# Gathered activations spread between gathered rows, eight row buffers and seven load buffers in a two-layer decoder trunk

## The chip, the cores and the metric

The kernel runs as one program on one core of a Trainium2 chip. The metric is device microseconds of one execution; the time before is the median of three runs. The profiler recorded one further execution, and its trace is what is read below. Engine names are those of the profile: PE is the matrix engine and PEld its weight loads, DVE the vector engine, ACT the scalar engine, POOL the GpSimd engine, SP the sync engine, which here issues nearly all weight loads from DRAM.

## The reference

Two layers, 256 tokens, width 1024, all float32. Each layer has a mixing part (projection, windowed attention, a short convolution, a gated mixer, output projection) and a retrieval part called PEER. The change lies in PEER:

```python
def block(t):                                   # t: tokens x 1024
    q = (t @ w_pq).reshape(T, 8, 2, 128)
    s = einsum('thpk,hpnk->thpn', q, sub_keys)  # two times 128 key scores per head
    # top 16 of each half, top 16 of the 256 sums: 8 heads x 16 experts per token
    gate = softmax(best_s)
    u = expert_down[experts]                    # 16384 experts of 1024
    act = gelu(einsum('td,thkd->thk', t, u))
    vv = expert_up[experts]
    return einsum('thk,thkd->td', gate * act, vv)
x = x + gate2 * peer_ffn(h2)
```

## The kernel before

**Two ways to sum the experts.** Instead of gathering 128 experts for each of 256 tokens, the kernel streams both expert tables, 128 tiles of 128 experts each, through the PE. The *first product* multiplies every `down` tile with all 256 tokens and leaves GELU activations for all experts. For the first `T` = 192 tokens a gate for every expert is made from one-hot matrices (`make_onehots`, `gate_mm`), and the gated activations `acts` stay in SBUF. The *second product* (`combine`) streams the 128 `up` tiles and accumulates `acts` times `up` in four PSUM banks.

**The last 64 tokens.** For the other `TS` = 64 tokens the second product covers only part of the work in matrix form: their ungated activations are written to DRAM (`act_rows`) in the first product. In the second product POOL issues, for each of 64 steps k, an indirect DMA that gathers one expert row of 1024 floats on each of 128 partitions (`fetch`, 512 KB, a *row* below), and another that gathers 64 activations on each partition (`fetch_acts`, 32 KB, an *act* below). For every group of eight acts DVE makes eight weights (`weights`, three instructions), and for every row it does one multiply and add over 128x1024 (`add_row`).

**Order in the second product.** It is written by hand (a manual schedule); elsewhere the compiler's scheduler sets the order on each engine. The PE works through tile i with ten matmuls of 128x512, six with the high part of the split `up` tile and four with its low part. Ahead of it ACT casts the raw tile to its high part (`hi`), and DVE subtracts to get the low part (`lo`); `hi` and `lo` have three buffers each, so both run about two tiles ahead of the PE. Every fourth tile, `split` prepares four tiles of `acts`: two casts on ACT and one subtraction on DVE. In the same DVE queue stand the row additions, spread evenly from tile `F_FIRST` to tile `F_LAST` by `want`, and the weights. DVE, POOL and PE each take their queue in order, so an addition that waits for its row holds up the `lo` behind it, and with it the PE.

**Buffers.** Raw tiles of all weight streams share one pool of `RAW` = 5 buffers, which SP refills in order (`dma_ahead`). Rows have `RING` = 4 buffers, so the fetch of row k + 4 stands behind the addition of row k. Acts have two halves of eight. POOL's queue at that place is: 4 rows, 24 acts, then eight rows and eight acts in turn. In layer 0, at tile 84, `tables` also puts three loads and a masking instruction for the next layer into the POOL queue, and at tile 92 the residual stream is read back from DRAM on it.

Of the kernel before, what the change touches and what calls it, by code (L numbers as in the profile page):

```python
# [11 lines left out]
F16 = mybir.dt.float16  # L12
# [5 lines left out]
P = 128  # L18
# [11 lines left out]
NP = 64  # L30
RAW = 5
AHEAD = 300
# [12 lines left out]
TS = S - T  # L45
RING = 4
GROUP = 8
F_FIRST = 9
F_LAST = 126
# [8 lines left out]
def hybrid_trunk(ctx: ExitStack, tc: tile.TileContext, x_in, c_in, vec_in, w_ada, w_in, w_out, w_pq,  # L58
# [82 lines left out]
    R_T = region(64 * S, 2, D)  # L141
    R_ROWS = region(96 * S, RING, D)
    R_SUM = region(112 * S, D)
# [769 lines left out]
    def experts(layer, rest):  # L913
# [3 lines left out]
        def make_onehots(g):  # L917
            tile4 = work.tile([P, 4, 4 * P], F16, name="oh", tag="oh", bufs=2)
            oh = tile4[:, 0].rearrange("p (i n) -> p i n", i=4)
# [59 lines left out]
        def split(q):  # L979
# [3 lines left out]
            for i in range(4 * q, 4 * q + 4, n):  # L983
# [6 lines left out]
                for k in range(n):  # L990
                    splits[i + k] = hi[:, k, :P], lo[:, k, :P], slot[:, k, T + P:2 * T + TS]

        def combine(layer, late):

# [5 lines left out]
            acc = {p: bank("acc", 4) for p in turns}  # L1000
            rows = up.rearrange("l j i c -> (l j i) c")
            where_act, where_row, w8 = (R_IX[:, n, :] for n in range(3))
            fetched = added = 0

            def fetch(k):
                nc.gpsimd.indirect_dma_start(  # L1006
                    out=R_ROWS[:, k % RING, :], out_offset=None, in_=rows,
                    in_offset=bass.IndirectOffsetOnAxis(ap=where_row[:, k:k + 1].bitcast(U32), axis=0))

            def fetch_acts(g):  # L1010

                for k in range(g * GROUP, (g + 1) * GROUP):
                    nc.gpsimd.indirect_dma_start(  # L1013
                        out=R_ACTS[:, k % (2 * GROUP), :], out_offset=None, in_=act_rows[layer][:, :],
                        in_offset=bass.IndirectOffsetOnAxis(ap=where_act[:, k:k + 1].bitcast(U32), axis=0))

# [8 lines left out]
            def add_row(k):  # L1025
                v = R_ROWS[:, k % RING, :]
                if k == 0:
                    nc.vector.tensor_scalar(R_SUM, v, w8[:, 0:1], None, op0=OP.mult)
                else:
                    nc.vector.scalar_tensor_tensor(R_SUM, v, w8[:, k:k + 1], R_SUM, op0=OP.mult, op1=OP.add)  # L1030
# [9 lines left out]
            split(0)  # L1040
            nc.vector.tensor_copy(where_act.bitcast(U32), pairs[:, 0, :])
            nc.vector.tensor_scalar(where_row.bitcast(U32), pairs[:, 0, :], float(layer * P * P), None, op0=OP.add)
            split(1)
            while fetched < RING:
                fetch(fetched)
                fetched += 1
            fetch_acts(0)
            fetch_acts(1)
            for i in range(128):
# [4 lines left out]
                while added < want(i):  # L1054
                    add_row(added)
                    added += 1
                    if fetched < TS:
                        fetch(fetched)
                        fetched += 1
                g = -(-want(i + 2) // GROUP) - 1  # L1060
                if i >= F_FIRST - 2 and g > -(-want(i + 1) // GROUP) - 1:
                    weights(g)
                    if 1 < g + 2 < TS // GROUP:
                        fetch_acts(g + 2)
                if i == 127 and layer + 1 < DEPTH:
# [61 lines left out]
        for i in range(128):  # L1127
# [21 lines left out]
            elif start is not None:  # L1149
# [3 lines left out]
                while sent < want and len(waiting) < 2:  # L1153
                    waiting.append((sent, gate_mm(sent)))
                    sent += 1
                    if made < NG:
                        make_onehots(made)
                        made += 1
            if j == 1:
                tdone = 4 * gdone  # L1160
                pend = (pair, act(pair, ps, tdone), tdone)
# [101 lines left out]
```

## Time and profile before

| What | Value |
|---|---|
| Median of the runs | 1806.55 us (three runs, 1805.11 to 1808.86) |
| The profiled execution | 1808.34 us, its span in the trace 1806.6 us |
| Granted PE clock, mean of the span | 0.987 |
| Busy share of the span | PE 96%, PEld 87%, DVE 79%, ACT 50%, POOL 48% |
| DRAM traffic | 454.48 MB, 252 GB/s on average |
| Second product of layer 0 | from 582.0 us to 916.3 us of the span |
| Second product of layer 1 | from 1468.1 us to 1795.5 us of the span |

The difference of 1.7 us between the execution's own time and its span lies before the first and after the last recorded instruction. A group's row in the page gives line, engine, operation, output and input by the program's names, count, busy time and mean duration, and the idle time ahead of it with what ended it. Many buffers are regions of one large tile named `arena`, so that name alone does not tell rows from acts: the line does (before, L1006 fetches rows, L1013 fetches acts, L1030 adds rows, L1021 to L1023 make weights, L229 makes `lo`, L236 makes `hi`, L989 is the subtraction of `split`, L1034 is the second product on the PE).

### The profile page before, as it was taken

How to read it: one execution, taken by the hardware profiler on the slowest of the kernel's cores; microseconds unless marked ns; L12 is line 12 of the kernel's file. 1: busy time of each engine (PE TensorE's matmuls, PEld its weight loads, DVE VectorE, ACT ScalarE, POOL GpSimd, SP SyncE). 2: the span in 40 equal slices, each digit the busy share in tenths (PEclk: the TensorE clock that was granted, in tenths of full speed). 3: DMA queues.
4: the chain of work that ended last, by engine and by line, in shares of the span. 5: the costliest groups of instructions: out<-in, count | busy, mean ns of one | idle time of the engine just before them, and what ended most of it. 6: DMA issues, size and time to landing. Idle time of an engine off the chain costs nothing.

```text
span 1806.6 us, 32055 instructions
## 1 busy us (share of the span) xinstructions
PE 1734.2 (96%) x11848; PEld 1578.5 (87%) x11848; DVE 1433.9 (79%) x2679; ACT 905.6 (50%) x1469; POOL 870.6 (48%) x697
## 2 busy tenths in 40 slices
PE   7999999999999899998999999999999997998898
PEld 6789999999999677776888999999999996877787
DVE  5868998888998588886966699957777857977896
ACT  2445455544445354554656555545544454545453
POOL 1000204779994765775400011317777746777641
PEclk9999999999999999998999999999999999999999
DMA  9865568887887798999943446666665677988895
GB/s 368 309 230 175 172 209 283 263 261 252 259 262 242 254 328 320 330 320 332 365 153 127 164 164 186 201 194 200 191 201 190 197 258 247 338 305 316 317 389 189
DMA packets 159279, 454.48 MB, mean 252 GB/s; under 512 B 50513, under 2 KB 50897, under 8 KB 157970
## 3 DMA queue, kind: packets, MB, share of 16 engines
q1 hardware_dynamic: 99936, 363.38, 59.0%
q0 software_dynamic: 23936, 80.50, 12.2%
q10 hardware_dynamic: 35250, 8.56, 2.2%
q8 instruction: 93, 1.52, 0.3%
q14 instruction: 64, 0.52, 0.1%
HBM read 440.75 MB, written 11.54 MB: 250 GB/s over the span
## 4 chain that ended last, share of the span: by engine, by line
PE 76%; DVE 9%; issue 5%; DMA 4%; POOL 4%; ACT 1%; SPq 0%; DVEq 0%; POOLq 0%; ACTq 0%
PE acc L1034 22%; PE ch L308 14%; PE ch L309 14%; PE ch L310 14%; POOL arena L1013 3%; DVE lo L229 3%; PE ch L306 2%; DMA arena<-in_up,arena 2%; PE g L938 1%; PE g L939 1%; PE ch L388 1%; DMA raw<-in_w_ada 1%; PE acc L308 1%; PE acc L310 1%; PE acc L309 1%
## 5 line engine op out<-in xcount | busy, mean ns | idle before, releaser
L236 ACT CAST hi<-raw 128x1024 fp32r<-128x1024 f32 x554 | 581.5, 1050 | 715.1 <-PE ch L310 367.2
L229 DVE TENSOR_TENSOR lo<-raw,hi 128x1024 fp32r<-128x1024 f32 x554 | 676.4, 1230 | 154.2 <-ACT hi L236 138.5
L308 PE MATMUL ch<-hh,hi 128*128 128x256 f32 x2336 | 666.1, 285 | 0.0
L309 PE MATMUL ch<-hh,lo 128*128 128x256 f32 x2336 | 658.6, 282 | 0.2 <-DVE lo L229 0.2
L310 PE MATMUL ch<-hh,hi 128*128 128x256 f32 x2336 | 657.8, 282 | 0.0
L925 POOL TENSOR_SCALAR oh<-iota,picks 128x128 f16<-128x128 f16 x384 | 429.8, 1136 | 258.1 <-issue 148.3
L309 PEld LDWEIGHTS ch<-hh,lo 128*128 128x128 f32 x2336 | 440.3, 188 | 0.8 <-DVE lo L229 0.6
L308 PEld LDWEIGHTS ch<-hh,hi 128*128 128x128 f32 x2336 | 439.8, 188 | 0.3 <-issue 0.3
L310 PEld LDWEIGHTS ch<-hh,hi 128*128 128x128 f32 x2336 | 439.9, 188 | 0.0
L1034 PE MATMUL acc<-hi,hh 128*128 128x512 f32 x1536 | 411.6, 403 | 19.3 <-DVE hh L989 17.0
L1034 PEld LDWEIGHTS acc<-hi,hh 128*128 128x128 f32 x1536 | 295.4, 193 | 91.8 <-DVE hh L989 19.2
L1034 PE MATMUL acc<-lo,hh 128*128 128x512 f32 x1024 | 288.5, 403 | 27.9 <-DVE lo L229 27.9
L1006 POOL DMA_INDIRECT arena<-in_up,arena x128 | 193.2, 1509 | 199.6 <-DVE arena L1030 126.7
L1034 PEld LDWEIGHTS acc<-lo,hh 128*128 128x128 f32 x1024 | 196.4, 193 | 78.6 <-DVE lo L229 33.1
L1030 DVE SCALAR_TENSOR_TENSOR arena<-arena 128x1024 f32<-128x1024 f32 x126 | 161.6, 1283 | 79.5 <-DMA arena<-in_up,arena 79.5
L1013 POOL DMA_INDIRECT arena<-act_rows,arena x128 | 204.3, 1596 | 40.6 <-issue 33.5
L194 DVE SCALAR_TENSOR_TENSOR raw<-raw,arena 128x1024 f32<-128x1024 f32 x96 | 117.2, 1223 | 16.6 <-DMA raw<-in_w_ada 10.7
L784 POOL CAST arena<-arena 128x512 f16<-128x512 uint32 x32 | 29.2, 926 | 139.8 <-DVE arena L773 108.0
L748 POOL DMA_DIRECT2D arena<-in_keys x2 | 1.1, 563 | 155.5 <-DVE ra L324 100.8
L930 DVE TENSOR_TENSOR oh<-oh,parts 128x512 f16<-128x512 f16 x192 | 75.9, 438 | 0.0
L928 DVE TENSOR_TENSOR oh<-iota,parts 128x512 f16<-128x512 f16 x96 | 41.5, 434 | 35.5 <-PE g L939 29.5
L989 DVE TENSOR_TENSOR hh<-arena,hh 128x768 fp32r<-128x768 f32 (+1 forms) x66 | 61.3, 929 | 0.6 <-ACT hh L987 0.3
(232 smaller groups left out, 1602.4 us busy)
## 6 DMA issues: line engine op xcount, KB each, us to landing
raw<-in_down SPq DMA_DIRECT2D x256, 512.0 KB
raw<-in_up SPq DMA_DIRECT2D x256, 512.0 KB
raw<-in_w_ada SPq DMA_DIRECT2D x96, 512.0 KB
raw<-in_w_pq SPq DMA_DIRECT2D x32, 512.0 KB
raw<-in_w_in SPq DMA_DIRECT2D x26, 512.0 KB
raw<-in_w_out SPq DMA_DIRECT2D x16, 512.0 KB
act_rows<-ungated ACTq DMA_DIRECT2D x128, 64.0 KB
arena<-in_w_in SPq DMA_DIRECT2D x6, 512.0 KB
```

What stands on the lines that cost most here:

```text
L194: op = nc.vector.scalar_tensor_tensor(raw, raw, 1.0, cact, op0=OP.mult, op1=OP.mult, accum_out=mods[layer][:, col:col + 1])
L229: nc.vector.tensor_sub(lo, raw, hi.bitcast(F32))
L236: nc.scalar.copy(hi, raw)
L308: nc.tensor.matmul(dst, hi[:, cols], k[0], start=start, stop=False, **kw)
L309: nc.tensor.matmul(dst, lo[:, cols], k[0], start=False, stop=False, **kw)
L310: nc.tensor.matmul(dst, hi[:, cols], k[1], start=False, stop=stop, **kw)
L925: nc.gpsimd.tensor_scalar(oh[:, i, :], iota, picks[:, t:t + 1], None, op0=OP.is_equal)
L930: nc.vector.tensor_tensor(og[j], on, wide(1 + j), op=OP.mult)
L1006: nc.gpsimd.indirect_dma_start(out=R_ROWS[:, k % RING, :], out_offset=None, in_=rows, in_offset=bass.IndirectOffsetOnAxis(ap=where_row[:, ...
L1013: nc.gpsimd.indirect_dma_start(out=R_ACTS[:, k % (2 * GROUP), :], out_offset=None, in_=act_rows[layer][:, :], in_offset=bass.IndirectOffse ...
L1030: nc.vector.scalar_tensor_tensor(R_SUM, v, w8[:, k:k + 1], R_SUM, op0=OP.mult, op1=OP.add)
L1034: nc.tensor.matmul(acc[piece], w, u[:, lo:hi], start=piece not in opened, stop=last, skip_group_check=True)
```

## The change

- An act is fetched behind each row: step k issues row k + 4 (later k + 8) and then act k + 16. The first 16 acts are fetched in a run at the start of the second product.
- The first four rows are fetched in the first product, in code that stands at its tile 108, together with the two small DVE instructions (`where`) that make the addresses.
- Rows have four buffers up to tile 24 and eight from there on. The four new ones lie where the `acts` of the first 22 tiles were, which `split` has used up by then; at tile 24 four more rows are fetched at once.
- The two one-hot buffers move from the work pool into the arena, where the row sum and the acts lie later. The room in the pool goes to two more raw buffers, seven in place of five.
- The additions begin at tile 10 in place of 9.

```diff
-RAW = 5
+RAW = 7
-RING = 4
-F_FIRST = 9
+F_FIRST = 10
-    R_ROWS = region(96 * S, RING, D)
+    R_ROWS = [region(at * S, D) for at in (96, 100, 104, 108, 0, 4, 8, 12)]
+    R_ON = [region(at * S, D).bitcast(F16).rearrange("p (k c) -> p k c", k=4) for at in (112, 116)]
...
         def make_onehots(g):
-            tile4 = work.tile([P, 4, 4 * P], F16, name="oh", tag="oh", bufs=2)
+            tile4 = R_ON[g % 2]
...
+        free = deque(range(4))
+        slots = []
+        def fetch():
+            k = len(slots)
+            if free and k < TS:
+                slots.append(free.popleft())
+                nc.gpsimd.indirect_dma_start(
+                    out=R_ROWS[slots[k]], out_offset=None, in_=rows,
+                    in_offset=bass.IndirectOffsetOnAxis(ap=where_row[:, k:k + 1].bitcast(U32), axis=0))
+        def fetch_act(k):
+            if k < TS:
+                nc.gpsimd.indirect_dma_start(
+                    out=R_ACTS[:, k % (2 * GROUP), :], out_offset=None, in_=act_rows[layer][:, :],
+                    in_offset=bass.IndirectOffsetOnAxis(ap=where_act[:, k:k + 1].bitcast(U32), axis=0))
...
         def combine(layer, late):
             split(0)
-            nc.vector.tensor_copy(where_act.bitcast(U32), pairs[:, 0, :])
-            nc.vector.tensor_scalar(where_row.bitcast(U32), pairs[:, 0, :], float(layer * P * P), None, op0=OP.add)
             split(1)
-            while fetched < RING:
-                fetch(fetched)
-                fetched += 1
-            fetch_acts(0)
-            fetch_acts(1)
+            for k in range(2 * GROUP):
+                fetch_act(k)
...
                 while added < want(i):
                     add_row(added)
+                    free.append(slots[added])
+                    fetch()
+                    fetch_act(added + 2 * GROUP)
                     added += 1
-                    if fetched < TS:
-                        fetch(fetched)
-                        fetched += 1
+                if i == 24:
+                    free.extend(range(4, 8))
+                    for _ in range(4):
+                        fetch()
                 if i >= F_FIRST - 2 and g > -(-want(i + 1) // GROUP) - 1:
                     weights(g)
-                    if 1 < g + 2 < TS // GROUP:
-                        fetch_acts(g + 2)
...
         # first product
+            if i == 108:
+                where()
+                for _ in range(4):
+                    fetch()
```

How this moves the queues. POOL, layer 0, from the end of the retrieval part to the first rows of the second product, before (L883 saves the residual stream, L784 and L925 serve the retrieval and the one-hots, L1006 fetches a row, L1013 an act):

```order
L883 DMA x_dram<-arena 128x2048
L784 CAST arena<-arena 128x512 x16
L925 TENSOR_SCALAR oh<-iota,picks 128x128 x192
L1006 DMA arena<-in_up,arena 128x1024 x4
L1013 DMA arena<-act_rows_102,arena 128x64 x24
L1006 DMA arena<-in_up,arena 128x1024 x8
L1013 DMA arena<-act_rows_102,arena 128x64 x8
```

And now (L1007 fetches a row, L1014 an act):

```order
L883 DMA x_dram<-arena 128x2048
L784 CAST arena<-arena 128x512 x16
L925 TENSOR_SCALAR arena<-iota,picks 128x128 x12
L1007 DMA arena<-in_up,arena 128x1024 x4
L925 TENSOR_SCALAR arena<-iota,picks 128x128 x180
L1014 DMA arena<-act_rows_102,arena 128x64 x16
L1007 DMA arena<-in_up,arena 128x1024
L1014 DMA arena<-act_rows_102,arena 128x64
```

The scheduler puts the first four rows much earlier than tile 108, behind the first 12 of 192 one-hot instructions; the second product opens with 16 acts, and from there row and act alternate, where 24 acts stood in a run.

POOL, layer 0, around the loads for the next layer (L458 to L463), before:

```order
L1006 DMA arena<-in_up,arena 128x1024 x8
L1013 DMA arena<-act_rows_102,arena 128x64 x8
L1006 DMA arena<-in_up,arena 128x1024 x2
L458 DMA arena<-in_rel_bias 128x2048
L459 DMA arena<-in_sgu_w 128x512
L460 DMA arena<-in_sgu_b 128x256
L461 AFFINE_SELECT arena<-arena 128x512
L463 MEMSET arena 128x2x2
L1006 DMA arena<-in_up,arena 128x1024 x4
```

And now:

```order
L1007 DMA arena<-in_up,arena 128x1024
L1014 DMA arena<-act_rows_102,arena 128x64
L458 DMA arena<-in_rel_bias 128x2048
L459 DMA arena<-in_sgu_w 128x512
L460 DMA arena<-in_sgu_b 128x256
L461 AFFINE_SELECT arena<-arena 128x512
L463 MEMSET arena 128x2x2
L1007 DMA arena<-in_up,arena 128x1024
```

The loads stand at the same tile; around them rows and acts alternate, and the first fetch behind them is that of row 50, which waits for the addition of row 42.

DVE, layer 0, where the addresses are made (`where`; L1041 and L1042 before, L999 and L1000 now). Before, at the start of the second product, between the subtractions of `split` (L989):

```order
L229 TENSOR_TENSOR lo<-raw,hi 128x1024
L989 TENSOR_TENSOR hh<-arena,hh 128x2x192 x2
L1041 CAST arena<-pairs 128x64
L1042 TENSOR_SCALAR arena<-pairs 128x64
L989 TENSOR_TENSOR hh<-arena,hh 128x4x192
L974 TENSOR_TENSOR arena<-arena,gt 128x384
```

And now, early in the first product, at the end of the retrieval part (L850 makes the expert numbers `chosen`, from which ACT and a small DMA make `pairs`):

```order
L229 TENSOR_TENSOR lo<-raw,hi 128x1024
L850 SCALAR_TENSOR_TENSOR chosen<-arena 128x128
L229 TENSOR_TENSOR lo<-raw,hi 128x1024
L194 SCALAR_TENSOR_TENSOR raw,mod_109<-raw,arena 128x1024
L855 COPY picks<-g 128x128
L229 TENSOR_TENSOR lo<-raw,hi 128x1024
L859 SCALAR_TENSOR_TENSOR parts<-g,parts 128x128
L999 CAST arena<-pairs 128x64
L1000 TENSOR_SCALAR arena<-pairs 128x64
```

The two instructions moved ahead by most of the first product, to a place shortly behind the DMA that they wait for.

More of the change, by code (lines that the diff above doesn't have):

```diff
@@ L991, in split, with where @@
                     splits[i + k] = hi[:, k, :P], lo[:, k, :P], slot[:, k, T + P:2 * T + TS]
+        rows = up.rearrange("l j i c -> (l j i) c")
+        where_act, where_row, w8 = (R_IX[:, n, :] for n in range(3))
+        free = deque(range(4))
+        slots = []
+        def where():
+            nc.vector.tensor_copy(where_act.bitcast(U32), pairs[:, 0, :])
+            nc.vector.tensor_scalar(where_row.bitcast(U32), pairs[:, 0, :], float(layer * P * P), None, op0=OP.add)
+        def fetch():
[10 more added lines that the diff above has]
+                    in_offset=bass.IndirectOffsetOnAxis(ap=where_act[:, k:k + 1].bitcast(U32), axis=0))
         def combine(layer, late):
@@ L1000, in combine @@
             acc = {p: bank("acc", 4) for p in turns}
[L1001 to L1015, printed above, removed]
+            added = 0
             def weights(g):
@@ L1025, in add_row @@
             def add_row(k):
-                v = R_ROWS[:, k % RING, :]
+                v = R_ROWS[slots[k]]
                 if k == 0:
```

## The prediction

> **What bounds the kernel now.** I read the windows by stage first, then the waits and the PE's timeline within the stage that loses time. The first answer below counts the second product's matmuls alone (length of the window, PE busy and count, PEld, granted clock, DMA share, GB/s). The second is the PE's timeline at a stretch without loss (start of a tile's first group, 28 tiles apart) and at one stall.
>
> ```profile
> 582.00:916.30 334.30, 309.22 (x1278) 246.73 (x1278) 0.96 0.89 316
> 1468.10:1795.50 327.40, 305.11 (x1276) 243.75 (x1276) 0.97 0.86 309
> 846.00:912.00 66.00, 66.00 (x285) 53.52 (x284) 1.00 0.94 345
> ```
>
> ```profile
> 846.71 1.55 PE L1034 MATMUL acc<-hi,hh 128*128 128x512 f32 x6
> 911.77 1.55 PE L1034 MATMUL acc<-hi,hh 128*128 128x512 f32 x6
> ...
> 707.04 0.63 PE L1034 MATMUL acc<-hi,hh 128*128 128x512 f32 x2
> 711.83 2.08 PE L1034 MATMUL acc<-hi,hh 128*128 128x512 f32 x4 [4.16 <-DVE hh L989]
> ```
>
> A tile of ten matmuls takes (911.77 - 846.71) / 28 = 2.324 us when nothing is late. At that pace the windows would last 1278 x 0.2324 = 297.0 us and 1276 x 0.2324 = 296.5 us. They last 334.3 and 327.4, so 37.3 + 30.9 = 68.2 us are lost, part of it as a lower granted clock behind each stall (0.96 and 0.97, against 1.00 in the stretch without loss; the four matmuls at 711.83 take 2.08 us). The other stages hold nearly full PE work and are the same before and after. The waits of both stages, layer 0 first, name the cause:
>
> ```profile
> POOL arena L1006 <- DVE arena L1030: 64.3, 32, 5.7
> DVE arena L1030 <- DMA arena<-in_up,arena: 39.7, 6, 7.5
> DVE arena L1021 <- DMA arena<-act_rows,arena: 6.1, 1, 6.1
> ...
> DVE arena L1030 <- DMA arena<-in_up,arena: 39.8, 7, 8.5
> DVE arena L1021 <- DMA arena<-act_rows,arena: 6.1, 1, 6.1
> ```
>
> DVE waits 45.8 us in layer 0 and 45.9 us in layer 1 for rows and acts; of these 91.7 us the PE loses 68.2, or 0.74 of each, since `lo` runs some two tiles ahead. Why rows are late stands in POOL's timeline (the run of eight acts, then the rows) and DVE's:
>
> ```profile
> 685.39 1.80 POOL L1013 DMA_INDIRECT arena<-act_rows,arena  x1 [0.30 <-DVE arena L1023]
> ...
> 698.59 0.95 POOL L1013 DMA_INDIRECT arena<-act_rows,arena  x1 [0.30 <-issue]
> 699.84 1.96 POOL L1006 DMA_INDIRECT arena<-in_up,arena  x1 [0.30 <-DVE arena L1030]
> 704.59 0.94 POOL L1006 DMA_INDIRECT arena<-in_up,arena  x1 [0.30 <-issue]
> 709.62 1.28 DVE L1030 SCALAR_TENSOR_TENSOR arena<-arena 128x1024 f32<-128x1024 f32 x1 [7.50 <-DMA arena<-in_up,arena]
> ```
>
> For 14.45 us POOL issues acts that nobody needs yet, while four additions free the four row buffers. The next row goes out at 701.80 and DVE can add it at 709.62, 7.8 us later. Yet POOL is idle for 64.3 us of that stage, waiting for additions.
>
> **The change, part by part.** *Rows behind rows.* The additions now cover 64 rows in 116 tiles, one per 116 / 64 x 2.324 = 4.21 us. POOL must issue one row and one act in that time. What an issue costs beside a busy DVE I take from the ten runs of eight acts, each window reaching to the next row's issue (the sum, and the fastest and slowest):
>
> ```profile
> 1570.92:1585.36 14.44, 12.00 (x8) 1.00 0.89 325
> 1645.52:1666.56 21.04, 18.59 (x8) 1.00 0.92 321
> sum 175.30, POOL 150.92; mean POOL 15.09
> ```
>
> That is 175.30 / 80 = 2.19 us each (1.81 to 2.63), so 4.38 us for a pair, 0.17 us more than a row's interval. From row 4 to row 47 (behind it there are no acts left to fetch) POOL falls back 44 x 0.17 = 7.5 us. The four extra rows at tile 24 add 4 x 2.19 = 8.8 us, together 16.3 us. With eight buffers a row is issued 8 x 4.21 = 33.7 us ahead of its addition; its own issue (2.2) and landing (7.8) leave 23.7 us, so 7.4 us remain. With four buffers, up to tile 24, the lead is 16.8 us, which leaves 6.8 us at row 4 and 5.4 at row 12. So the 79.5 us of row waits go; I keep 1 us a layer for the first eight rows (0 by the mean price; at 2.63 us an issue row 12 comes 8 x 1.05 - 6.4 = 2 us late) and 1.5 us a layer for landings later than 7.8 (an issue-to-landing above it is not bounded by any row here; the longest single wait is 8.5 us).
>
> *The first acts.* They stood behind four rows, which now land in the first product, so POOL starts them 8.3 us earlier, limited by the last write of `act_rows`:
>
> ```profile
> 583.34 1.78 POOL L1006 DMA_INDIRECT arena<-in_up,arena  x1 [18.33 <-DVE arena L1042]
> 591.67 0.95 POOL L1013 DMA_INDIRECT arena<-act_rows,arena  x1 [0.30 <-issue]
> ```
>
> ```profile
> 583.77 1.34 DMA act_rows<-ungated
> ```
>
> The second answer is the chain of waits, with that write: it lands at 585.1, so the acts come 6.5 us earlier, and the weights are wanted one tile, 2.3 us, later: the wait of 6.1 us goes.
>
> *The loads for layer 1 in POOL's queue.* They hold it from 819.48 to 832.25, 12.8 us, in layer 0 alone, and the rows behind them were late:
>
> ```profile
> 819.48 0.60 POOL L458 DMA_DIRECT2D arena<-in_rel_bias  x1
> 828.31 3.74 POOL L461 TENSOR_SCALAR_AFFINE_SELECT arena<-arena 128x512 f32<-128x512 f32 x1 [7.11 <-DMA arena<-in_sgu_w]
> 832.25 1.02 POOL L1006 DMA_INDIRECT arena<-in_up,arena  x1 [0.16 <-issue]
> ```
>
> They come at row 50, where by the mean price 7.4 us are left: short by 5.4 us, 4 us on the PE; by the fastest price (3.62 us a pair) POOL has no arrears and nothing is short. I take 3, between 0 and 4.
>
> *DVE becomes the next limit to look at*, since nothing holds it back any more. Its pitches, from layer 1's timeline:
>
> ```profile
> 1753.76 1.28 DVE L1030 SCALAR_TENSOR_TENSOR arena<-arena 128x1024 f32<-128x1024 f32 x1
> 1754.95 0.68 DVE L1021 TENSOR_TENSOR arena<-arena,fold 128x512 f32<-128x512 f32 x1
> ...
> 1756.47 0.95 DVE L989 TENSOR_TENSOR hh<-arena,hh 128x768 fp32r<-128x768 f32 x1
> 1757.34 2.35 DVE L229 TENSOR_TENSOR lo<-raw,hi 128x1024 fp32r<-128x1024 f32 x2
> 1759.61 1.28 DVE L1030 SCALAR_TENSOR_TENSOR arena<-arena 128x1024 f32<-128x1024 f32 x1
> ```
>
> From start to start a row takes 1.19 us, weights 1.52, a split 0.87, a `lo` 2.27 / 2 = 1.135. Per tile that is 1.135 + 1.19 x 64/116 + 0.87/4 + 1.52 x 8/116 = 2.11 us, 91% of 2.324: it does not bind, and the stretch from 846 to 912, with all of these in it, loses nothing. *Transfers*: the first window moved 334.3 us x 316 GB/s = 105.6 MB; in some 300 us that needs 352 GB/s, and the page's best slice has 389:
>
> ```profile
> GB/s 368 309 230 175 172 209 283 263 261 252 259 262 242 254 328 320 330 320 332 365 153 127 164 164 186 201 194 200 191 201 190 197 258 247 338 305 316 317 389 189
> ```
>
> *Moved to the first product*: two DVE instructions and four rows a layer. Each layer's POOL has a gap there, behind its first twelve one-hots, that takes four issues of 2.2 us, and nothing on the PE waits for it:
>
> ```profile
> 321.94 5.57 POOL L925 TENSOR_SCALAR oh<-iota,picks 128x128 f16<-128x128 f16 x4 [28.90 <-issue]
> 1208.26 3.57 POOL L925 TENSOR_SCALAR oh<-iota,picks 128x128 f16<-128x128 f16 x4 [34.18 <-issue]
> ```
>
> DVE may wait there for the small DMA of `pairs`, by estimate about as long as the 1.34 us of the `act_rows` write, with the `lo` of two tiles made ahead: nothing. The one-hots' new place changes no instruction: nothing. *Seven raw buffers* let SP run further ahead. Outside the second product that can help only where loads are waited for, in the first mixing part:
>
> ```profile
> DVE raw L194 <- DMA raw<-in_w_ada: 9.0, 8, 4.2
> PE ch L306 <- DMA raw<-in_w_in: 2.5, 2, 1.8
> ```
>
> Gain 0 to 11.5 us; I take 2, near the PE's own row, since DVE is not the bound there. It may cost a little, too, where more loads in flight delay a row or the scheduler's order shifts: down to -3.
>
> Sum: 68.2 - 2 x (1 + 1.5) - 3 + 2 = 62 us. From the profiled execution's 1808.34 that gives 1746; that execution is 1.8 us above the median of 1806.55, which gives 1744.5. I say 1745.
>
> **The rivals.** *A, the forecast*: 1735 to 1757 (no stall left and the raw buffers' gain doubled; or 12 us more of waits).
>
> *B, POOL is only just too slow.* At 2.45 us an issue, between mean and slowest run, a pair takes 4.9 us. The arrears are 44 x 0.69 + 9.8 = 40.2 us against 23.7 of slack: DVE waits 16.5 us a layer and 12.8 more in layer 0, 45.8 us, of which the PE loses 34: 1806.5 - 68 + 34 - 2 = 1770. For it: DVE will be busier than in the ten runs, parts of which fell into DVE's waits, where an issue is cheap:
>
> ```profile
> 1691.67 3.17 POOL L1013 DMA_INDIRECT arena<-act_rows,arena  x1 [0.30 <-DMA arena<-act_rows,arena]
> 1695.14 4.03 POOL L1013 DMA_INDIRECT arena<-act_rows,arena  x1 [0.30 <-issue]
> 1706.57 0.94 POOL L1006 DMA_INDIRECT arena<-in_up,arena  x1 [0.30 <-issue]
> ```
>
> At 1706.57 DVE stood still and the issue took 0.94 us; the other two ran beside a DVE without gaps. Against it: any new wait of DVE makes issues cheap again.
>
> *C, slower: POOL becomes the bound.* The same place at a price that decides: with c for a pair, DVE's waits are 2 x (44 x (c - 4.21) + 2c - 23.7) + 12.8, and 0.74 of them outweigh 68 + 2 us from c = 5.4, or 2.7 us an issue, just above the slowest run. At 2.9 us it would be 95 us of PE loss, 1832. Against it: that price would have to hold on average while DVE waits 129 us. The Trainium skill (SBUF — State Buffer, section "SBUF: two separate sides") has a rule that speaks for C: while DVE holds the port that it shares with GpSimd, GpSimd can't write descriptors, and its DMAs starve. The trace agrees in kind, with 0.94 us beside an idle DVE and up to 4.03 beside a busy one. The same page's figures (section "A bandwidth-pool intuition that's wrong": 620 ns alone, 3100 ns beside DVE, a factor of 5) would by estimate make 4.7 us of 0.94, a pair of 10 us and some 380 us of loss where the sum has a gain of 62; the ten runs bear out a factor of two.
>
> *D, transfers bind.* If no more than the 345 GB/s of the window from 846 can be had, layer 0 takes 105.6 MB / 345 = 306 us, 9 us above its floor; layer 1's 101 MB fit. The time would be 1745 + 9 = 1754. Against it: 389 GB/s in one slice.
>
> **How the numbers follow.** A 0.67, B 0.20, D 0.08, C 0.05. The point is A's, 1745. The range reaches down to 1732 (68.2 us all gone, and 6 us from the raw buffers) and up to 1775, past B and D. A run counts as the same within 0.2%, 3.6 us, about what can be told here. Only C is on the other side: slower 0.05; the same 0.01, between B and C; faster 0.94.
>
> **What would show it.** Right: DVE's row waits fall from 79.5 us to under 10, its act waits from 12.2 to none; the two windows shrink to about 299 and 302 us with clock 0.99; POOL's issues average about 1.9 us, and POOL's wait for additions shrinks from 64.3 us in layer 0 to a few. B or C: row waits spread over rows 30 to 50, POOL without a gap there. D: DMA share at 0.97 or more, and ACT waiting for raw tiles. The forecast is wrong if an issue beside a DVE without stalls costs more than 2.4 us on average, or a row takes well over 8 us to land once SP has seven loads in flight.

## The result and the profile after

| What | Before | After |
|---|---|---|
| Median, measured side by side | 1805.83 us (four runs, 1804.70 to 1808.86) | 1743.68 us (four runs, 1742.29 to 1744.19) |
| Ratio, 95% interval | | 0.9652 (0.9635 to 0.9669) |
| Profiled execution, its span | 1808.34 us, 1806.6 us | 1742.29 us, 1740.6 us |
| Granted PE clock, mean of the span | 0.987 | 0.998 |

The change makes the kernel 62 us faster; 1745 was forecast. Two slow executions, one of e7 (4372.62 us) and one of the kernel before beside e1 (1816.41 us), count in the medians of the experiments but not in their ratios. The windows of the second product's matmuls in the changed kernel (same columns as before: length, PE busy and count, PEld, clock, DMA share, GB/s) answer to the first two lines of the prediction:

```profile
582.00:879.00 297.00, 296.70 (x1277) 240.69 (x1278) 1.00 0.94 348
1432.80:1729.30 296.50, 296.41 (x1276) 240.34 (x1276) 1.00 0.89 330
```

These 1277 and 1276 matmuls (1278 and 1276 in the windows of before) take 297.0 and 296.5 us where they took 334.3 and 327.4: the floor that the prediction worked out, at full clock. They alone keep the PE busy for all but 0.3 and 0.1 us. The ends of these windows were set to hold that many matmuls; without a choice of window, from the start of the first to that of the last of all 1280 matmuls of a layer, the time fell from 336.8 to 299.5 us and from 330.3 to 299.4. The waits of the two stages, layer 0 first:

```profile
POOL arena L1007 <- DVE arena L1041: 30.1, 23, 3.0
POOL arena L1014 <- issue: 17.7, 58, 0.3
POOL arena L461 <- DMA arena<-in_sgu_w: 8.7, 1, 8.7
...
POOL arena L1007 <- DVE arena L1041: 47.4, 34, 3.0
DVE arena L1032 <- DMA arena<-act_rows,arena: 0.3, 1, 0.3
```

No line of DVE waiting for a gathered row is left, and 0.3 us of waiting for acts; POOL waits for additions (L1041), so it has time over. The page's groups say what an issue costs, before (L1006 rows, L1013 acts) and after (L1007 rows, L1014 acts; L1041 is the row addition, the last column its idle time ahead):

```profile
L1006 POOL DMA_INDIRECT arena<-in_up,arena x128 | 193.2, 1509 | 199.6 <-DVE arena L1030 126.7
L1013 POOL DMA_INDIRECT arena<-act_rows,arena x128 | 204.3, 1596 | 40.6 <-issue 33.5
```

```profile
L1007 POOL DMA_INDIRECT arena<-in_up,arena x128 | 181.3, 1417 | 112.3 <-DVE arena L1041 77.5
L1014 POOL DMA_INDIRECT arena<-act_rows,arena x128 | 182.0, 1422 | 85.0 <-PE acc L1045 46.8
L1041 DVE SCALAR_TENSOR_TENSOR arena<-arena 128x1024 f32<-128x1024 f32 x126 | 162.1, 1286 | 0.0
```

An issue lasts 1.42 us, 1.72 with the gap of 0.30 ahead of the next one; a pair takes 3.44 us of the 4.21 between two rows. The chain that ended last is now PE for 90% of the span:

```profile
PE 90%; DVE 7%; DMA 1%; ACT 1%; issue 0%; SPq 0%; DVEq 0%; ACTq 0%
```

One stage became slower. Counted from the trace's start times of matmuls, the first product from its first gates on (2250th to 4300th matmul and 8200th to 10000th) took 423.2 us, both layers together, before and takes 426.6 now, without a wait of the PE in either. The windows of the instructions on its result `ch` (length, then PE, PEld, DVE and ACT busy with their counts, clock, DMA share, GB/s), before and after, show the same busy PE with fewer matmuls in it:

```profile
360.00:540.00 180.00, 169.88 (x1374) 164.75 (x1373) 0.00 (x0) 19.87 (x84) 1.00 0.80 258
```

```profile
360.00:540.00 180.00, 169.68 (x1363) 164.64 (x1362) 0.00 (x0) 20.15 (x84) 1.00 0.79 256
```

Eleven matmuls fewer in 180 us, with 264 gate matmuls beside them in both, is 0.8% of pace. By those start times the account of the two profiled executions is: second products -36.8 and -30.4 us, first mixing part (up to the 800th matmul) -1.6, first product +3.4, the rest -0.7; sum -66.1.

### The profile page after: what moved, and what is told of

It reads as the page before. It is cut to its first block, busy times and chain, and to the rows that moved or that the text cites. A ratio compares the mean times of both kernels' runs of the same rounds, so it can differ in the third digit from the quotient of the medians.

```text
span 1740.6 us, 32293 instructions
## 1 busy us (share of the span) xinstructions
PE 1716.8 (99%) x11848; PEld 1573.4 (90%) x11848; DVE 1435.0 (82%) x2679; ACT 906.9 (52%) x1469; POOL 835.3 (48%) x697
## 4 chain that ended last, share of the span: by engine, by line
PE 90%; DVE 7%; DMA 1%; ACT 1%; issue 0%; SPq 0%; DVEq 0%; ACTq 0%
PE acc L1045 34%; PE ch L308 15%; PE ch L309 14%; PE ch L310 14%; PE ch L306 3%; DVE lo L229 2%; PE g L938 1%; PE g L939 1%; PE ch L388 1%; DMA raw<-in_w_ada 1%; PE acc L308 1%; PE acc L310 1%; PE acc L309 1%; DVE arena L770 1%; DVE arena L771 1%; DVE arena L769 1%
## 5 line engine op out<-in xcount | busy, mean ns | idle before, releaser
L925 POOL TENSOR_SCALAR arena<-iota,picks 128x128 f16<-128x128 f16 x384 | 431.0, 1139 | 238.0 <-PE g L939 110.3
L1045 PE MATMUL acc<-hi,hh 128*128 128x512 f32 x1536 | 400.1, 395 | 0.0
L1045 PEld LDWEIGHTS acc<-hi,hh 128*128 128x128 f32 x1536 | 289.3, 188 | 67.3
L1045 PE MATMUL acc<-lo,hh 128*128 128x512 f32 x1024 | 280.9, 395 | 0.0
L1007 POOL DMA_INDIRECT arena<-in_up,arena x128 | 181.3, 1417 | 112.3 <-DVE arena L1041 77.5
L1014 POOL DMA_INDIRECT arena<-act_rows,arena x128 | 182.0, 1422 | 85.0 <-PE acc L1045 46.8
L1041 DVE SCALAR_TENSOR_TENSOR arena<-arena 128x1024 f32<-128x1024 f32 x126 | 162.1, 1286 | 0.0
L930 DVE TENSOR_TENSOR arena<-arena,parts 128x512 f16<-128x512 f16 x192 | 77.0, 441 | 31.2 <-PE g L938 31.2
L784 POOL CAST arena<-arena 128x512 f16<-128x512 uint32 x32 | 29.2, 925 | 139.5 <-DVE arena L773 108.0
L949 ACT ACTIVATE arena<-g 128x344 f32<-128x344 f32 (+23 forms) x96 | 31.2, 325 | 73.6 <-DVE arena L946 72.5
L989 DVE TENSOR_TENSOR hh<-arena,hh 128x768 fp32r<-128x768 f32 (+1 forms) x66 | 61.6, 934 | 1.1 <-ACT hh L987 1.1
```

The lines of the kernel that those rows point to most:

```text
L925: nc.gpsimd.tensor_scalar(oh[:, i, :], iota, picks[:, t:t + 1], None, op0=OP.is_equal)
L930: nc.vector.tensor_tensor(og[j], on, wide(1 + j), op=OP.mult)
L1007: nc.gpsimd.indirect_dma_start(out=R_ROWS[slots[k]], out_offset=None, in_=rows, in_offset=bass.IndirectOffsetOnAxis(ap=where_row[:, k:k + ...
L1014: nc.gpsimd.indirect_dma_start(out=R_ACTS[:, k % (2 * GROUP), :], out_offset=None, in_=act_rows[layer][:, :], in_offset=bass.IndirectOffse ...
L1045: nc.tensor.matmul(acc[piece], w, u[:, lo:hi], start=piece not in opened, stop=last, skip_group_check=True)
```

## The experiments

Each row is one kernel; the last three columns are taken from start times in its trace: the second product of layer 0 (4300th to 5750th matmul), that of layer 1 with the end (from the 10000th on), and the first product from the gates on, both layers. The second product's own matmuls are the 4553rd to the 5852nd and the 10529th to the 11828th, so its two columns also hold the end of the first product ahead of it. Kernels of one group ran on one chip beside the kernel before, whose median stands in the group's line.

| Kernel | Median us | Ratio to before, 95% | 2nd, layer 0 | 2nd, layer 1 | 1st |
|---|---|---|---|---|---|
| before | 1805.83 | | 343.6 | 392.2 | 423.2 |
| after | 1743.68 | 0.9652 (0.9635 to 0.9669) | 306.8 | 361.8 | 426.6 |
| *before here: 1804.46* | | | | | |
| e1 after again | 1744.76 | 0.9687 (0.9645 to 0.9729) | 306.8 | 361.8 | 426.6 |
| e2 five raw buffers | 1745.78 | 0.9700 (0.9656 to 0.9744) | 306.8 | 361.8 | 427.1 |
| e3 and one-hots in the pool | 1741.18 | 0.9674 (0.9631 to 0.9717) | 307.5 | 361.4 | 423.7 |
| e4 spread acts alone | 1751.76 | 0.9724 (0.9682 to 0.9767) | 314.6 | 365.5 | 423.2 |
| *before here: 1806.69* | | | | | |
| e5 four row buffers | 1744.79 | 0.9667 (0.9626 to 0.9708) | 306.9 | 361.8 | 426.6 |
| e6 acts in runs | 1760.49 | 0.9754 (0.9712 to 0.9795) | 316.6 | 368.1 | 426.6 |
| e7 acts twice | 1822.39 | 1.0078 (1.0047 to 1.0108) | 346.7 | 400.6 | 426.6 |
| e8 one-hots in own tiles | 1745.50 | 0.9669 (0.9638 to 0.9701) | 306.8 | 361.8 | 427.1 |
| *before here: 1800.24* | | | | | |
| e9 gates in pairs | 1755.42 | 0.9749 (0.9725 to 0.9773) | 307.0 | 364.2 | 435.1 |
| e10 late rows | 1752.26 | 0.9730 (0.9702 to 0.9758) | 310.9 | 365.1 | 426.6 |
| e11 pairs and pool | 1772.57 | 0.9835 (0.9809 to 0.9862) | 310.5 | 368.3 | 447.3 |
| *before here: 1805.42* | | | | | |
| e12 two parts alone | 1741.01 | 0.9651 (0.9626 to 0.9676) | 308.4 | 361.3 | 423.7 |

**Which part makes the gain.** e1 is the changed kernel unedited.

> The changed kernel as it is, beside the three that follow, so that all four are read against each other. The median should be 1742 to 1745 us (0.965 of before). In its trace the second product takes 295 us in both layers without a wait of DVE for rows or acts, and the 256-element matmuls of the first product start every 119.7 to 119.8 ns from the place on where one-hots are made, where the kernel before had 118.7.

1744.76, as expected; its stretches are those of the changed kernel. (The 295 us of this and the next expectations is no stretch of the table: at 0.2324 us it would be some 1270 matmuls.) e4 spreads the acts in the kernel before and leaves the rest as it was:

```diff
-RAW = 7
+RAW = 5
-F_FIRST = 10
+F_FIRST = 9
-            tile4 = R_ON[g % 2]
+            tile4 = work.tile([P, 4, 4 * P], F16, name="oh", tag="oh", bufs=2)
-                if i == 24:
-                    free.extend(range(4, 8))
...
-            if i == 108:
-                where()
...
             split(0)
+            where()
             split(1)
+            for _ in range(4):
+                fetch()
```

> The kernel before with one part of the change: from row 4 on an act is fetched behind each row, 16 acts at the start. Four row buffers, the first rows fetched at the start of the second product, five raw buffers, one-hots in the work pool, additions from tile 9. Theory 1, the order of the issues is the cause: with four buffers the lead is 16.8 us, of which issue (1.4) and landing (7.8) leave 7.6, so the row waits of 79.5 us fall to under 10; the first acts still come late in both layers (6.1 us of DVE, 4.5 of PE each) and the loads for layer 1 hold POOL for 12.8 us against 7.6 (4 us of PE). 1806 - 68 + 9 + 4 = 1751, between 1745 and 1757. Theory 2, the eight row buffers are needed for it, since at 2.19 us an issue a pair takes longer than a row's interval of 4.21 us: rows fall back 0.17 us each and the loads cost their full 12.8, and with the early rows missing too 1765 to 1785.

1751.76: theory 1. The order of issues alone brings 52.7 of the 59.7 us that the changed kernel gains on this chip, with the old four buffers. What it leaves is in its waits: in layer 0 (the lines below) the first acts, row 6 with 5.2 us at the start, and 3.4 us for two rows behind the loads for layer 1; in layer 1 another 6.5 us ahead of the first weights.

```profile
DVE arena L1041 <- DMA arena<-in_up,arena: 8.6, 3, 5.2
DVE arena L1032 <- DMA arena<-act_rows,arena: 5.8, 1, 5.8
```

e5 takes the eight row buffers from the changed kernel, e10 the early first rows (same edit as the last two parts of e4):

```diff
-                if i == 24:
-                    free.extend(range(4, 8))
-                    for _ in range(4):
-                        fetch()
```

> The changed kernel with four row buffers to the end: the spread acts, the early first rows, seven raw buffers and the one-hots' place stay. The lead of a row is 16.8 us, of which an issue (1.42 in the changed kernel's trace) and the landing (7.8) leave 7.6 us. Theory 1, an issue costs what the changed kernel's trace has: no wait but at the loads for layer 1, which hold POOL 12.8 us, 5.2 us too long, some 4 us of PE: 1745 to 1749 us. Theory 2, rows fall back as at 2.19 us an issue (0.17 us each, used up near row 40): a few us of waits in both layers besides, 1752 to 1762.

> The changed kernel with the first four rows and their addresses fetched at the start of the second product again; the rest stays. Theory 1, the acts stand behind the four rows and come 6 us later: DVE waits some 6 us for the first weights in each layer, the PE loses 4 to 4.5 of it, 1749 to 1754 us. Theory 2, the one tile of delay (2.3 us, additions from tile 10) and cheaper issues already cover most of it: 1743 to 1747 us.

e5: 1744.79, just under theory 1's range. Its two waits in layer 0, behind the loads, are 4.2 us where 5.2 were expected, and where theory 1 had 4 us of PE they cost next to nothing (306.9 against 306.8; 300.0 against 299.5 from the first matmul to the last):

```profile
DVE arena L1041 <- DMA arena<-in_up,arena: 4.2, 2, 2.3
```

So four more row buffers bring next to nothing once the acts are spread. e10: 1752.26, in theory 1's range; the waits for the first acts are back with 5.1 us (the line) and 4.7 us, and the second products take 4.1 and 3.3 us more. But theory 1 named only the acts: rows 5 and 6 of layer 0 (the second line) and row 4 of layer 1 come late too, by 4.3 and 3.7 us, so the early rows save both waits.

```profile
DVE arena L1032 <- DMA arena<-act_rows,arena: 5.1, 1, 5.1
DVE arena L1041 <- DMA arena<-in_up,arena: 4.3, 2, 2.9
```

e6 keeps the eight buffers and fetches the acts in runs of eight again:

```diff
-                    fetch_act(added + 2 * GROUP)
...
                     weights(g)
+                    for k in range((g + 2) * GROUP, (g + 3) * GROUP):
+                        fetch_act(k)
```

> The changed kernel with the acts fetched in runs of eight again, a run behind each set of weights as before the change; eight row buffers from tile 24 on, the early rows and the rest stay. Theory 1, the run of eight (14.4 us of POOL and up to 21) is harmful only as long as it exceeds the lead left to a row: with four buffers 7.6 us are left, with eight 24.5. So from tile 24 on nothing waits, and the runs ahead of it (two of them) cost some 7 us of DVE each, 5 of PE: 10 us a layer, 1755 to 1765 us. Theory 2, the order alone makes the gain and the buffers do nothing for it: the row waits of 40 us a layer come back and the time is 1795 to 1805.

1760.49, theory 1: DVE waits for rows twice in layer 0, 7.0 us at the start and the line below between 640 and 700 us, and from 700 us on, with eight buffers, not at all; in layer 1 it waits 7.3 and 4.4 us, nothing later than 1540 us. Spreading and buffering are two cures for the same run: spreading alone took 52.7 us off (e4), buffering with the early rows 46.2 (1806.69 - 1760.49), or 55.6 and 51.1 us by the second products' stretches, and with the acts spread the buffers add next to nothing (e5).

```profile
DVE arena L1041 <- DMA arena<-in_up,arena: 7.3, 1, 7.3
```

**When POOL does become the bound.** e7 fetches each act from the 17th on a second time, to a place that nobody reads:

```diff
                     fetch_act(added + 2 * GROUP)
+                    fetch_act(added + 2 * GROUP, R_SPARE, GROUP)
```

> The changed kernel with every act from the 17th on fetched a second time to a place that nobody reads: three issues a row in place of two, 48 times a layer, to see what an issue costs when POOL is short of time. Theory 1, an issue lasts 0.94 us where it finds the port free and else the rest of the DVE instruction that is under way plus 0.82 us, so 1.42 us on average and 2.1 at the most (1.72 from issue to issue): a row takes 5.2 us against the interval of 4.21, the rows fall back 45 us in 48 rows and the buffers cover 17.6 of them, so some 25 us of DVE waits a layer, fewer where waits make issues cheap: 1760 to 1790 us. Theory 2, the price of the prediction, 2.19 us: 6.57 us a row, some 95 us of DVE waits a layer, 1870 to 1890. If POOL is not short at all (0.94 us an issue once they stand in a queue), 1742 to 1746.

1822.39, between the two. Its windows of the second product, its waits of layer 0 and its row of the page for acts:

```profile
582.00:923.00 341.00, 309.25 (x1279) 244.86 (x1280) 0.97 0.88 309
1480.00:1816.00 336.00, 305.80 (x1261) 239.64 (x1259) 0.97 0.84 294
```

```profile
DVE arena L1042 <- DMA arena<-in_up,arena: 54.9, 20, 7.6
```

```profile
L1015 POOL DMA_INDIRECT arena<-act_rows,arena x224 | 315.9, 1410 | 113.7 <-issue 61.2
```

The price of an issue is theory 1's (1.41 us, though from row 4 to row 47 POOL never rests for more than 0.31 us between two issues). The waits are twice theory 1's upper 25 us: 54.9 in layer 0 and 54.9 in layer 1. By the start times, rows 5 to 47 are added every 4.79 and 4.96 us, near three issues of 1.41 + 0.30 = 5.13 and above the interval of 4.21. The buffers' slack, which I had put at 17.6 us, is used up early: in layer 0 the time from the end of a row's issue to its addition is 5.8 us at row 13, where DVE has waited already; the four extra rows lift it to 15.1 at row 17, and at row 22 it is 6.6 and DVE waits again. This is rival C's mechanism at work: some 5 us of POOL for a row, and the kernel is 0.8% slower than before. The second products' 39.9 and 38.8 us over the changed kernel's are 0.72 of the DVE waits, the 0.74 of the prediction.

**Why the first product is slower.** e2 takes back the raw buffers, e3 the one-hots' place too, e8 gives the one-hots two tiles of their own:

```diff
-RAW = 7
+RAW = 5
```

> The changed kernel with five raw buffers in place of seven, the one-hots still in the arena (the room of the two buffers stays empty). Theory 1, the one-hots' place in the arena makes the first product slower: the pitch stays at 119.8 ns there, only the small gain of the first mixing part (2 us) goes, 1744 to 1746 us. Theory 2, the seven raw buffers make it slower, by transfers that run further ahead or by where hi and lo come to lie: the pitch goes back to 118.7, some 4 us less, and the gain of the first mixing part goes, some 2 us more, 1740 to 1742 us. Under both the second product stays at 295 us: its gain doesn't hang on raw buffers. If it grows to 299 us or more, seven buffers carried part of that gain.

```diff
-RAW = 7
+RAW = 5
-            tile4 = R_ON[g % 2]
+            tile4 = work.tile([P, 4, 4 * P], F16, name="oh", tag="oh", bufs=2)
```

> The changed kernel with five raw buffers and the one-hots back in the work pool, as before the change. Both theories of the slower first product (the one-hots' place, the seven raw buffers) expect the pitch of 118.7 ns again, some 4 us less than the changed kernel there, and the gain of the first mixing part gone, some 2 us more: 1740 to 1742 us. If the pitch stays at 119.8 ns, neither is the cause and the four early rows or the address instructions remain. The second product stays at 295 us.

```diff
-RAW = 7
+RAW = 5
+    oh_tiles = [consts.tile([P, 4, 4 * P], F16, name=f"oht{n}") for n in range(2)]
-            tile4 = R_ON[g % 2]
+            tile4 = oh_tiles[g % 2]
```

> The changed kernel with five raw buffers and the one-hots in two tiles of their own, outside the arena and not drawn from the pool, so that their waits are set slice by slice as in the arena, at addresses near those of before. The matmuls of the first product show two paces in the runs so far, 118.6 and 120.0 ns from start to start, and which of them holds changes only at a break; with one-hots in the arena it is mostly 120.0 from the first gates on, with one-hots in the pool 118.6. Theory 1, the address in the arena decides: 118.6 ns, 1740 to 1742 us as with the pool. Theory 2, the waits and signals of the finer tracking decide, by the moment at which a gate group ends: mostly 120.0 ns, 1744 to 1746.

e2 and e8 came out at 1745.78 and 1745.50 (theory 1 of e2, theory 2 of e8), e3 at 1741.18. The same window of `ch` in e2, e3 and e8:

```profile
360.00:540.00 180.00, 169.39 (x1359) 164.18 (x1358) 0.00 (x0) 20.16 (x84) 1.00 0.80 256
```

```profile
360.00:540.00 180.00, 169.88 (x1373) 164.60 (x1371) 0.00 (x0) 20.67 (x87) 1.00 0.80 259
```

```profile
360.00:540.00 180.00, 169.60 (x1360) 164.59 (x1361) 0.00 (x0) 20.00 (x84) 1.00 0.80 256
```

With one-hots in the pool the pace of before is back (1373); in the arena or in tiles of their own it isn't (1359, 1360). In the arena it is the slower one with five raw buffers (1359) as with seven (1363), so the seven are not its cause; the pool was tried with five only. e2 and e3 differ in the one-hots' place alone (427.1 and 423.7 us in the stage), so that place is the cause, and by e8 it is not the arena's address: tiles that aren't drawn from the pool have the slower pace at both places tried. That their finer waits and signals do it, as theory 2 of e8 has it, is argued by elimination and not shown. The timelines show how it looks from one matmul to the next behind a run of eight gates, in the changed kernel and in e3:

```profile
421.63 0.22 PE L939 MATMUL g<-arena 128*128 128x128 f16 x1
421.65 0.36 PE L308 MATMUL ch<-hh,hi 128*128 128x256 f32 x1
421.86 0.29 PE L309 MATMUL ch<-hh,lo 128*128 128x256 f32 x1
421.98 0.28 PE L310 MATMUL ch<-hh,hi 128*128 128x256 f32 x1
422.10 0.29 PE L308 MATMUL ch<-hh,hi 128*128 128x256 f32 x1
```

```profile
420.69 0.22 PE L939 MATMUL g<-oh 128*128 128x128 f16 x1
420.72 0.36 PE L308 MATMUL ch<-hh,hi 128*128 128x256 f32 x1
420.92 0.27 PE L309 MATMUL ch<-hh,lo 128*128 128x256 f32 x1
421.03 0.28 PE L310 MATMUL ch<-hh,hi 128*128 128x256 f32 x1
421.15 0.29 PE L308 MATMUL ch<-hh,hi 128*128 128x256 f32 x1
```

In nanoseconds of start times, the changed kernel goes on here with steps of 120 to the next gates (119 and 121 in turn behind most others, mean 120.0), e3 with 115, 117, 122, 120, 119 (mean 118.6). A few nanoseconds at the restart (from the first matmul to the second 200 here, 202 in e3) go with one rhythm or the other in most stretches, and the rhythm then holds until the next break. They don't decide it by themselves: at 488.2 us of e9 a restart of 200 leads to 118.7. e9 and e11 tried to choose the rhythm by sending gates two groups at a time:

```diff
-                if want < NG and i % 2:
+                if want < NG and (i % 2 or want - sent < 2):
                     want = sent
```

> The changed kernel (seven raw buffers, one-hots in the arena) with the gates sent two groups at a time, so that more of them stand on the PE in runs of sixteen matmuls (27 runs of sixteen and 12 of eight over both layers, some split, where there were 14 and 68). In the traces so far a run of eight gates leaves the 256-element matmuls behind it at 120.0 ns where the one-hots lie in the arena or in tiles of their own, at 118.9 where they lie in the pool; a run of sixteen leaves them at 118.9 in both. Theory 1, what a gate run leaves behind sets the pace till the next break: the first product gets most of its 4 us back, 1739 to 1742 us. Theory 2, the place or the tracking of the one-hots slows the matmuls as such: 1743 to 1746 us, 120.0 ns behind runs of sixteen too.

> The version with five raw buffers and the one-hots in the pool, with the gates sent two groups at a time (29 runs of sixteen and 16 of eight, some split, where there were 13 and 64). Theory 1, what a gate run leaves behind sets the pace: the pace was 118.6 to 118.9 ns there already, so pairs change nothing beyond a microsecond, 1739 to 1743 us. Theory 2, fewer breaks are worth something by themselves: 1736 to 1739 us.

Both theories missed: 1755.42 and 1772.57. In e9 the quicker rhythm followed nine of the eleven runs of sixteen between the 2250th and the 4300th matmul, and the layer-1 stage from the 9000th to the 10000th matmul fell from 110.9 to 110.4 us. But the pairs cost more than that: gates now wait for POOL's one-hots, as e9's waits in the first product of layer 0 show. In e11 the PE's matmuls wait 18.9 us so, over both layers. The second products proper stay at 299.5 and 299.4 us from first to last matmul in both kernels, so what their columns have over the changed kernel's lies in the first product too.

```profile
PEld L938 <- POOL arena L925: 9.3, 15, 1.0
PE g L938 <- POOL arena L925: 6.7, 15, 0.8
```

**The version that is left.** e12 is e3 with four row buffers (the edit of e5): spread acts, early first rows and the additions from tile 10, whose start one tile later was not tried by itself.

> Two parts of the change alone: the acts spread behind the rows, and the first four rows with their addresses in the first product. Four row buffers to the end, five raw buffers, the one-hots in the pool. Theory 1, these two carry the whole gain and the pool's place avoids the slower pace of the first product: second products at about 307 and 362 us (the stretch counted from the 4300th and the 10000th matmul) as with eight buffers, 118.6 ns in the first product, 1740 to 1743 us, 3 us under the changed kernel as it is. Theory 2, eight row buffers and seven raw buffers cover each other, so that one alone could be left out and not both: 1745 to 1752.

1741.01 us, as theory 1 said. Its trace has one row wait, in layer 0:

```profile
DVE arena L1041 <- DMA arena<-in_up,arena: 4.3, 1, 4.3
```

Layer 0's second product is 1.6 us longer than the changed kernel's, the first product 2.9 us shorter. e3 and e12 are 3.6 and 3.8 us under e1; e12 ran in another group, and e3's runs (1739.27 to 1745.71) overlap e1's (1743.66 to 1745.04), so "not slower, with less" is shown, and the 3 us by the first product's stage rather than by the totals.

## Why the prediction was right, point by point

- **The loss and its cause**: right. 68.2 us were lost in the second product to rows and acts that came late; 37.3 + 30.9 came back as 334.3 - 297.0 and 327.4 - 296.5, that is 37.3 + 30.9. e4 and e10 split it: about 53 us by the order of issues, 7.4 by the early rows, which save a wait for rows as well as the one for acts.
- **POOL's price, and with it the residual**: mis-sized. The term 2.19 us was the pitch within ten runs of eight acts; the page's own means of all 128 were 1.51 and 1.60 us, and with the gap of 0.30 a pair by these is 3.71, inside the interval of 4.21. Measured: 1.42, a pair 3.44. POOL doesn't fall back, so the 1 and 1.5 us a layer and the 3 us for the loads, 8 us in all, were none. By the start times the lead of a row (end of its issue to its addition) never falls under 8.4 us from row 4 on, reaches 32, and drops from 30.4 to 18.5 at the loads.
- **The eight buffers**: credited with a slack of 23.7 us that e5 shows nobody needed; the landing of 7.8 us taken for every row was the long end, since e5's first row behind the loads was added 4.1 us after its issue.
- **The first acts**: right. Their wait is gone, 6.1 to 0.3 us at most, and back in e10.
- **DVE**: right, it doesn't bind. DVE waits for no row, is busy for 266.6 us of the first window's 297.0 (90%, where 91% was worked out), and the PE runs at its floor.
- **Transfers (rival D)**: not borne out; the first window moved 348 GB/s, the page's best slice 394:

```profile
GB/s 381 341 234 175 163 210 278 304 262 253 257 250 262 240 344 392 383 352 383 325 149 122 170 162 182 202 248 197 196 188 197 192 194 283 378 394 347 375 368 114
```

- **Moved to the first product**: right. DVE waits 0.5 and 2.6 us there for `pairs`, where 1.34 was estimated, and the PE waits for nothing near it.
- **Seven raw buffers, +2 us**: 1.6 us in the profiled run. It can't be told from nothing: the stretch up to the 800th matmul takes 148.4 us before, 146.9 and 147.9 us in two traces of the changed kernel, 148.3 with five buffers (e2), and 145.8 with five and the one-hots in the pool (e3).
- **"The one-hots' new place changes no instruction: nothing"**: wrong, 3.4 us, and with it that the other stages are the same before and after. The order of instructions told nothing of it; the cost is in the pace between them.
- **The point, hit to 1.3 us, is partly luck**: 8 us of residual that didn't come and 3.4 us that nobody expected pull opposite ways, and the profiled executions indeed lie 66 us apart where the sum had 62. The medians lie 62.2 apart, since the profiled execution of before is 2.5 us above the median of its four and that of after 1.4 us under.
- **Signs named beforehand**: row waits under 10 (0), act waits none (0.3), windows 299 and 302 (297.0 and 296.5), clock 0.99 (1.00) came. POOL's issues were to average 1.9 us and took 1.42, and POOL's wait for additions was to shrink from 64.3 to a few us; it is 30.1 in layer 0, the same error of price.
- **Rivals B and C** needed 2.45 and 2.7 us an issue. The last section says what an issue waits for, and why 1.42 is far from both.

## What to carry to other kernels

Work that a queue issues early is not free: a run of eight that nobody needs yet delays the one transfer that somebody waits for, and putting each small fetch behind the large one that frees its turn did as much as doubling the buffers and fetching the first rows early (55.6 against 51.1 us of the second products), with no buffer added. For an engine's price take the mean of all its instructions first, and a sample of its worst stretches as the bound. When a buffer moves from a rotating pool to a fixed place, compare the pace of the matmuls around it too, not only their order.

## What the runs showed of the hardware

**What an issue on POOL waits for.** POOL's issues and the DVE instructions beside them, in the changed kernel:

```profile
713.31 1.68 POOL L1007 DMA_INDIRECT arena<-in_up,arena  x1 [0.64 <-DVE arena L1041]
715.29 1.85 POOL L1014 DMA_INDIRECT arena<-act_rows,arena  x1 [0.31 <-issue]
719.50 0.95 POOL L1014 DMA_INDIRECT arena<-act_rows,arena  x1 [0.30 <-issue]
```

```profile
712.96 1.21 DVE L229 TENSOR_TENSOR lo<-raw,hi 128x1024 fp32r<-128x1024 f32 x1
715.10 1.23 DVE L229 TENSOR_TENSOR lo<-raw,hi 128x1024 fp32r<-128x1024 f32 x1 [0.92 <-ACT hi L236]
718.30 1.22 DVE L229 TENSOR_TENSOR lo<-raw,hi 128x1024 fp32r<-128x1024 f32 x1
```

The first `lo` ends at 714.17, the issue 0.82 later at 714.99; the second at 716.33 and 717.14, 0.81 later; the third ends 0.02 after its issue began, and that issue takes 0.95. In layer 0 of the changed kernel 84 issues began within a `lo`; of the 62 that began more than 0.12 us before its end, the middle half ended 0.81 to 0.82 us behind it. So as a rule an issue waits for the one DVE instruction that it meets and then needs 0.8 us: 0.94 to some 2.0, with a mean of 1.42 over those 84, as over all 256. Six of the 256 took 2.9 to 4.0 us. One of them, and DVE beside it:

```profile
745.77 4.04 POOL L1014 DMA_INDIRECT arena<-act_rows,arena  x1 [0.30 <-issue]
```

```profile
745.77 0.95 DVE L989 TENSOR_TENSOR hh<-arena,hh 128x768 fp32r<-128x768 f32 x1
746.64 2.35 DVE L229 TENSOR_TENSOR lo<-raw,hi 128x1024 fp32r<-128x1024 f32 x2
```

It ends at 749.81, 0.82 us behind the third of three DVE instructions that followed one another without a gap (748.99). All six ended 0.81 to 0.82 us behind the second or third instruction of such a run, and all six had begun within 15 ns after the first of the run; others that began so took 0.94 or 2.0 us, so what lets DVE go first again is open. Three issues of the changed kernel began within the reduction of `weights` (one input), 0.2 to 0.4 us before its end; they took 0.94 to 0.95 us and didn't wait (with the 0.81 us behind its end they would have taken 1.0 to 1.2). The Trainium skill (SBUF — State Buffer, section "Who interferes with whom") says that a DVE instruction with two SBUF inputs contends with a GpSimd instruction that reads SBUF, and that a reduction never does; the trace agrees in both. The Trainium skill infers in the same section that a `tensor_tensor`, which `lo` is, does not stall a DMA issued on GpSimd; here these issues waited for it, and the measurement decides. The factor of 5 that the Trainium skill has further up on that page (section "A bandwidth-pool intuition that's wrong"), for a copy, isn't seen with these instructions: 1.42 to 0.94 is 1.5.

**Two rhythms of the PE.** The 256-element matmuls of the first product, with a weight load each, no wait and the clock at 1.00, have two paces, 118.6 and 120.0 ns from start to start. Which holds is settled at a break and stays to the next; stretches of either are in the trace of the kernel before too. In a stage of some 425 us this is worth 3.4 us, more than the 1.9 us between the fastest and the slowest of the changed kernel's four runs. What at the break decides is open.
